# A hybrid RWKV-7/GLA layer on one core: the triangles of a head pair get their own products and their own tile

## The chip, the cores and the metric

The program runs on one core of a Trainium2 chip. The metric is the device time of one execution in microseconds. The engines are TensorE (PE, with its weight loads shown apart as PEld), VectorE (DVE), ScalarE (ACT), GpSimd (POOL) and the queue that issues the DMAs (SP).

## What is computed

One layer over 256 latent tokens and 256 context tokens of width 2048. After a modulated norm, one wide projection feeds two branches. The part that matters here is the RWKV-7 branch, 16 heads of width 64, in both directions:

```
def step(s, inp):                       # S <- S diag(w) + (S a) b^T + v k^T,  y = S r
    w_t, k_t, v_t, a_t, b_t = inp[:5]
    sa = jnp.einsum("bhvk,bhk->bhv", s, a_t)
    s = s * w_t[:, :, None, :] + sa[..., None] * b_t[:, :, None, :] + v_t[..., None] * k_t[:, :, None, :]
    y = jnp.einsum("bhvk,bhk->bhv", s, inp[5]) if emit else None
    return s, y
```

It runs over the context first and then, from the state reached, over the latents. Behind it come a norm per head, a gate, one projection for each branch (`w_a`, `w_b`), a gated sum, the output projection `w_out` and a last norm.

## The kernel before

**Three stages.** First the modulation, the wide projection and the GLA branch; then the RWKV-7 stage, which is what the change touches; then a tail that is almost only matmuls: 16 jobs with `w_b`, 16 with `w_a`, and `w_out`.

**The RWKV-7 stage.** The recurrence is done in chunks of 64 tokens, eight of them (0 to 3 context, 4 to 7 latent), for a pair of heads at a time; there are eight pairs, p = 0 to 7. Inside a chunk the recurrence is a unit lower triangular system, so each chunk, head and direction needs the inverse of a 64x64 triangle. For each pair there are these tracks:

- `fe_track`: the features: `kn`, `ar` (the a vectors and r, scaled), `bk` (the b vectors and k, scaled). Its second half starts when the products of the pair before are done (`("gg", p-1)`), and `ar` is written when `aq_track` of the pair before has read it.
- `gg_track`: the products of `bk` with `ar`, masked by DVE into `GM` (`pgc` for the context chunks, `pgl` for the latent ones). `GM` has two buffers, used by even and odd pairs. So each group of products waits for the scan two pairs back to have passed the chunks concerned (`past(p, i)`), the last one until its last chunk is done.
- `inv_track`: the inverses. ACT copies the triangles from `GM` into `Lin` (four copies), DVE transposes `Lin` into `M`, and POOL substitutes: 30 times a multiply into `tm` and an add into `M`, one after the other. Then DVE transposes `M` back into `Lin`, PE makes the off-diagonal block (`pH`, then `pZ`), and the result is copied into `Z`. It starts when `("gg", p)` is done.
- `aq_track`: DMAs that put part of `ar` into the rows of `GM` from which the triangles have been read.
- `sc_track`: the scan, eight steps. A step is `p1` on PE, a copy, `pU` on PE, a copy into `UV`, `pSs` on PE, then `Sn` on DVE and a copy. In the four latent steps PE adds to `pY`, and `mu`, a reduction of `pY` on DVE, ends the scan. Scans follow each other strictly, and scan p needs `Z` of pair p.

**What sets the order.** Tracks are generators. `Issue` keeps a clock for each engine from its own costs for each instruction, takes the track that can go first, and emits its instructions. So every engine has one fixed queue and works it off in that order. Between the small matmuls of the tracks it places dense ones, `acc` (three matmuls of 128x256 at a time: weights split in a high and a low part by ACT, `wH`, and DVE, `wL`): first the rest of the wide projection, and when the last pair's products and features are issued (`"C"`), the `w_b` jobs. What of the dense work finds no place beside the scans comes behind them.

The planner's price of a POOL operation is in `Op.__init__`; of the hand-over between two engines, in `LAT`:

```
            c = 35 + 0.83 * n if name == "memset" else 110 + 3.36 * n if name == "tensor_copy" else 149 + (
                1.667 if any(q == 0 and k > 1 for x in ins for q, k in x.ap[1:]) else 2.096) * n
```

Of the kernel before, what the change touches and what calls it, by code (L numbers as in the profile page):

```python
# [7 lines left out]
F32 = mybir.dt.float32  # L8
# [4 lines left out]
OP = mybir.AluOpType  # L13
# [4 lines left out]
P = 128  # L18
# [312 lines left out]
def hybrid_layer(tc, a, out):  # L331
    nc = tc.nc
    es = ExitStack()
    with es:
# [635 lines left out]
        def half(hd):  # L970
            return slice(64 * hd, 64 * hd + 64)
# [7 lines left out]
        def fe_track(p, fp, xp):  # L979

            yield lambda: p == 0 or ("feat", p - 1) in DONE
            wl = fp.tile([P, 2, 2, P], F32, name="wl", tag="wl", bufs=1)
            for i, nm in enumerate(("a_w2", "a_a2")):
                for hf in range(2):
                    Q.dma_start(wl[half(hf), i], a[nm][0][:, :, P * p:P * p + P].rearrange("d r c -> r d c"))
# [107 lines left out]
        def bt_track(p, d, bk):  # L1093
# [8 lines left out]
                rel(pt)  # L1102
            DONE.add(("bt", p) if ("bt", p, 1 - d) in DONE else ("bt", p, d))

        def gg_track(p, fp, xp):

            yield lambda: ("feat", p) in DONE
            s = RW[p]
            ar, bks = s["ar"], s["bks"]
            GM, GMr, BK = s["GM"], s["GMr"], s["BK"] = tuple(RW[n][p % 2] for n in ("GM", "GMr", "BK"))  # L1110
            left = [6]

            def done():
                left[0] -= 1
                if not left[0]:
                    DONE.add(("gg", p))

            def mask(m, n):
                return m[:, p % 2, None].to_broadcast([P, n, 2, 64])

            def ev_c(pg, hd):
                yield DV.tensor_tensor(GM[:, hd, 0:4], pg, mask(m_ab, 4), op=OP.mult)
                rel(pg)
                done()

            def ev_l(pg, hd, i):
                yield DV.tensor_tensor(GM[:, hd, 4 + i:6 + i], pg[:, :, :, 0, :], mask(m_ab, 2), op=OP.mult)
                yield DV.tensor_tensor(GMr[:, hd, i:i + 2], pg[:, :, :, 1, :], mask(m_r, 2), op=OP.mult)
                rel(pg)
                done()  # L1130

            yield past(p, 3)
            pg = []
            for hd in range(2):
                pg.append((yield Claim("g3", [P, 4, 2, 64], f"pgc{hd}", *bks, ar)))
            yield [PE.matmul(pg[hd][half(x), i, d, :], bks[d][half(hd), chunk(i, d), x, :], ar[half(hd), d, i, 0, :],
                             start=True, stop=True) for i in range(4) for d in range(2) for x in range(2) for hd in range(2)]
            for hd in range(2):
                iss.spawn(3, ev_c(pg[hd], hd), "evc")
            for i in (0, 2):  # L1140
                yield past(p, 5 + i)
                pg = []
                for hd in range(2):
                    pg.append((yield Claim("g3", [P, 2, 2, 2, 64], f"pgl{hd}", *bks, ar)))
                yield [PE.matmul(pg[hd][:, ii, d], bks[d][half(hd), chunk(4 + i + ii, d)].rearrange("p a b -> p (a b)"),
                                 ar[half(hd), d, i + ii, 1:3, :], start=True, stop=True)
                       for ii in range(2) for d in range(2) for hd in range(2)]
                for hd in range(2):
                    iss.spawn(3, ev_l(pg[hd], hd, i), "evl")

        def inv_track(p, fp, xp):

            yield lambda: ("gg", p) in DONE and (p < 2 or ("gi", p - 2) in DONE)
            s = RW[p]
            GM, Z = s["GM"], RW["Z"][p % 2]
            h0 = u0 = 64 * (p % 2)
            hs = slice(h0, h0 + 64)  # L1160
            qs = [slice(h0 + 32 * hd, h0 + 32 * hd + 32) for hd in range(2)]
            Lin, M, GMo = (RW[n][hs] for n in ("Lin", "M", "GMo"))
            for hd in range(2):
                for blk in range(2):
                    r = slice(u0 + 32 * blk, u0 + 32 * blk + 32)
                    cc = slice(32 * blk, 32 * blk + 32)
                    yield AC.copy(RW["Lin"][qs[hd]].rearrange("p t u -> p u t")[:, 16 * blk:16 * blk + 16, :],
                                  GM[r, hd, :, :, cc].rearrange("p i d t -> p (i d) t"))
            yield DV.transpose(M.rearrange("p i c -> p (i c)"), Lin.rearrange("p t u -> p (t u)"))
            for hd in range(2):  # L1170
                yield AC.copy(RW["GMo"][qs[hd]], GM[u0:u0 + 32, hd, :, :, 32:64].rearrange("p i d t -> p (i d) t"))
            iss.spawn(3, aq_track(p, xp), "aq")
            for j in range(1, 31):
                n = 31 - j
                tm = fp.tile([P, 256], F32, name="tm", tag="tm", bufs=2)
                tv = tm[hs, 0:n * j].rearrange("p (a b) -> p a b", b=j)
                yield PO.tensor_tensor(tv, M[:, j + 1:32, j:j + 1].to_broadcast([64, n, j]),
                                       M[:, j:j + 1, 0:j].to_broadcast([64, n, j]), op=OP.mult)
                yield PO.tensor_tensor(M[:, j + 1:32, 0:j], M[:, j + 1:32, 0:j], tv, op=OP.add)
            yield PO.memset(M.rearrange("p i c -> p (i c)")[:, ::33], 1.0)  # L1180
            yield DV.transpose(Lin.rearrange("p u c -> p c u"), M.rearrange("p i c -> p c i"))
            pH = yield Claim("g3", [P, 16, 32], "pH", Lin)
            hq = int(4)
            for u in range(0, 16, hq):
                yield [PE.matmul(pH[q, u + x, :], RW["GMo"][q, u + x, :], RW["Lin"][q, u + x, :], start=True, stop=True,
                                 tile_position=(q.start, q.start)) for x in range(hq) for q in qs]
            yield AC.copy(GMo, pH[hs])
            rel(pH)
            W = RW["Lin"].rearrange("p a b -> p (a b)").rearrange("p (i u) -> p u i", u=32)
            yield DV.transpose(W[hs].rearrange("p u i -> p i u"), M)  # L1190
            pZ = yield Claim("g3", [P, 16, 32], "pZ", GMo, Lin)
            for u in range(0, 16, hq):
                yield [PE.matmul(pZ[64 * hd:64 * hd + 32, u + x, :], RW["GMo"][qs[hd], u + x, :], W[qs[hd], 16 + u + x, :],
                                 start=True, stop=True, tile_position=(qs[hd].start, 64 * hd)) for x in range(hq) for hd in range(2)]
            yield lambda: p < 2 or ("sc1", p - 2) in DONE
            for hd in range(2):
                for blk in range(2):
                    r = slice(64 * hd + 32 * blk, 64 * hd + 32 * blk + 32)
                    yield (DV.tensor_copy if hd else AC.copy)(Z[r, :, 32 * blk:32 * blk + 32], W[qs[hd], 16 * blk:16 * blk + 16, :])
                yield (DV.tensor_copy if hd else AC.copy)(Z[64 * hd:64 * hd + 32, :, 32:64], pZ[64 * hd:64 * hd + 32])  # L1200
            rel(pZ)
            s["Z"] = Z
            DONE.add(("gi", p))

        def aq_track(p, xp):

            s = RW[p]
            ar, GM, rq = s["ar"], s["GM"], RW["rq"]
            us = rows(p)[0]
            for hd in range(2):  # L1210
                for g in range(2):
                    for d in range(2):
                        yield DM.dma_start(GM[us, hd, 4 * g:4 * g + 4, d, :], ar[half(hd), d, :, g, :])
                yield DM.dma_start(rq[us, :, :, hd, :], ar[half(hd), :, :, 2, :])
            DONE.add(("aq", p))

# [417 lines left out]
        fp = Pool(iss, fes.enter_context(tc.tile_pool(name="rwf", bufs=1, side="right", reuse_waits="tile")))  # L1634
        ies = ExitStack()
        ip = Pool(iss, ies.enter_context(tc.tile_pool(name="rwi", bufs=1, reuse_waits="tile")))
        for n, sh in (("Lin", [P, 32, 32]), ("M", [P, 32, 32]), ("GMo", [P, 16, 32])):
            RW[n] = iss.keep(ip.tile(sh, F32, name=n))
        RW["ar"] = iss.keep(xp.tile([P, 2, 4, 3, 64], F32, name="ar"))
        RW["rq"] = iss.keep(xp.tile([P, 2, 4, 2, 64], F32, name="rq"))  # L1640
        for n, sh in (("GM", [P, 2, 8, 2, 64]), ("BK", [P, 2, 8, 2, 64]), ("GMr", [P, 2, 4, 2, 64])):
            RW[n] = [iss.keep(xp.tile(sh, F32, name=f"{n}{i}")) for i in range(2)]
        RW["wlo"] = iss.keep(fp.tile([P, 2, 2, P], F32R, name="wlo"))
        G.memset(RW["wlo"].bitcast(F32), 0.0)
        RW["UV"] = iss.keep(xp.tile([P, 8, 2, 2, 64], F32, name="UV"))
# [4 lines left out]
        for p in range(8):  # L1650
            iss.spawn(3.2, fe_track(p, fp, xp), f"fe{p}")
            iss.spawn(3, v_track(p, ip), f"v{p}")
            iss.spawn(6, gg_track(p, ip, xp), f"gg{p}")
            iss.spawn(3, inv_track(p, ip, xp), f"inv{p}")
            iss.spawn(4, mv_track(p, ip, xp), f"mv{p}")
            iss.spawn(2, sc_track(p, xp), f"sc{p}")
# [129 lines left out]
```

## Time and profile before

| what | us |
|---|---|
| median of three runs (1376.9 to 1382.26) | 1380.76 |
| the profiled execution | 1380.07 |
| its span, first to last instruction | 1378.3 |
| PE busy | 1268.4 |
| DVE busy | 963.3 |
| POOL busy | 557.5 |

The span is what the trace shows; 1.8 us of the profiled execution lie around it. A busy time is the time in which the engine had an instruction running. The RWKV-7 stage lies between about 590 and 1213 us, the tail behind it.

### The profile page before, as it was taken

The page shows a single profiled execution, that of the slowest core. Times are in us where ns is not written, and L with a number is a line of the kernel's source. Part 1 is how long each engine was busy: PE and PEld are TensorE (multiplying, and loading weights), DVE is VectorE, ACT ScalarE, POOL GpSimd, SP SyncE. Part 2 cuts the span into 40 slices and gives each one's busy share as a digit, 9 for nine tenths or more (in the row PEclk, how much of TensorE's full clock was granted, in tenths as well). Part 3 has the DMA queues.
Part 4 walks back from the last instruction along what each step waited for, and adds up shares of the span by engine and source line. Part 5 has one row for each costly group of instructions (what it writes and reads, how often), then busy time and mean ns, then how long its engine had stood idle before and what let it go on. Part 6 is the DMA issues. An engine that isn't in the chain of part 4 may idle for free.

```text
span 1378.3 us, 29069 instructions
## 1 busy us (share of the span) xinstructions
PE 1268.4 (92%) x11223; PEld 1063.4 (77%) x11223; DVE 963.3 (70%) x2013; ACT 716.3 (52%) x1449; POOL 557.5 (40%) x684
## 2 busy tenths in 40 slices
PE   5999989999999999999888999798879899999996
PEld 3555579788788898998777778677768688899876
DVE  4433496875965747776986889579866876677656
ACT  5222244343434534486486767475847575544444
POOL 0000476776560000006785569547763855000002
PEclk9999999999999999999999999799989999999999
DMA  9999465455562533666543434243434253578574
GB/s 346 344 336 307 130 204 173 131 177 160 153 177 81 144 92 108 167 182 172 138 111 109 109 98 121 75 104 109 108 82 107 72 160 114 165 208 255 179 245 142
DMA packets 311182, 220.40 MB, mean 160 GB/s; under 512 B 37354, under 2 KB 286724, under 8 KB 310532
## 3 DMA queue, kind: packets, MB, share of 16 engines
q1 hardware_dynamic: 311044, 218.55, 54.4%
q8 instruction: 88, 1.44, 0.4%
q14 instruction: 50, 0.41, 0.1%
HBM read 199.76 MB, written 12.46 MB: 154 GB/s over the span
## 4 chain that ended last, share of the span: by engine, by line
PE 55%; DVE 17%; POOL 11%; ACT 7%; issue 5%; DMA 4%; SPq 1%; DVEq 0%; ACTq 0%; POOLq 0%
PE acc L304 35%; POOL M L304 6%; PE pv L304 6%; DVE wL L304 5%; POOL tm L304 5%; PE pg L304 3%; ACT Lin L304 2%; DMA raw<-in_w_out_dram 2%; ACT wH L304 2%; PE pS L304 1%; PE pout L304 1%; PE pgl L304 1%; DVE bk L304 1%; PE pU L304 1%; PE p L304 1%
## 5 line engine op out<-in xcount | busy, mean ns | idle before, releaser
L304 DVE TENSOR_TENSOR wL<-raw,wH 128x512 fp32r<-128x512 f32 x484 | 379.2, 792 | 166.3 <-ACT wH L304 157.8
L304 ACT CAST wH<-raw 128x512 fp32r<-128x512 f32 x484 | 293.9, 615 | 330.7 <-PE acc L304 204.4
L304 PE MATMUL acc<-lH,wH 128*128 128x256 f32 x896 | 287.6, 321 | 0.5 <-ACT tg L304 0.5
L304 PE MATMUL acc<-lH,wL 128*128 128x256 f32 x896 | 259.0, 289 | 0.9 <-DVE wL L304 0.9
L304 PE MATMUL acc<-lL,wH 128*128 128x256 f32 x896 | 258.9, 289 | 0.0
L304 POOL TENSOR_TENSOR tm<-M 64x30 f32<-64x30 f32 (+14 forms) x240 | 165.2, 688 | 153.0 <-DVE M L304 74.4
L304 PEld LDWEIGHTS acc<-lH,wH 128*128 128x128 f32 x896 | 177.0, 198 | 20.8 <-issue 5.7
L304 POOL TENSOR_TENSOR M<-M,tm 64x30 f32<-64x30 f32 (+14 forms) x240 | 180.0, 750 | 18.7
L304 PEld LDWEIGHTS acc<-lL,wH 128*128 128x128 f32 x896 | 177.6, 198 | 4.5 <-issue 3.0
L304 PEld LDWEIGHTS acc<-lH,wL 128*128 128x128 f32 x896 | 177.1, 198 | 1.3 <-DVE wL L304 1.3
L304 PE MATMUL acc<-hH,wH 128*128 128x512 f32 (+1 forms) x416 | 169.0, 406 | 1.0 <-ACT lo L304 1.0
L304 PE MATMUL acc<-hH,wL 128*128 128x512 f32 (+1 forms) x416 | 157.6, 379 | 0.0
L304 PE MATMUL acc<-hL,wH 128*128 128x512 f32 (+1 forms) x416 | 157.2, 378 | 0.0
L304 PEld LDWEIGHTS acc<-hH,wH 128*128 128x128 f32 x416 | 78.7, 189 | 38.0 <-issue 22.9
L304 POOL TENSOR_TENSOR gw<-gw,csl 128x512 f32<-128x512 f32 x60 | 73.7, 1229 | 64.7 <-DMA gw<-in_w_mod_dram 64.7
L304 POOL TENSOR_TENSOR xs<-yg,fg 128x512 f32<-128x512 f32 (+1 forms) x10 | 13.5, 1366 | 198.3 <-DVE yg L304 198.3
L304 PEld LDWEIGHTS acc<-hH,wL 128*128 128x128 f32 x416 | 78.8, 189 | 15.4 <-DVE wL L304 0.4
L304 POOL TENSOR_TENSOR ga<-ga,gw 128x512 f32<-128x512 f32 x60 | 86.0, 1434 | 4.2
L304 PEld LDWEIGHTS acc<-hL,wH 128*128 128x128 f32 x416 | 79.1, 190 | 10.5 <-DVE hL L304 0.4
L304 PE MATMUL acc<-yH,wH 128*128 128x256 f32 x256 | 76.2, 298 | 2.0 <-DVE mt L304 1.9
L304 PE MATMUL acc<-yH,wL 128*128 128x256 f32 x256 | 72.7, 284 | 0.0
L304 PE MATMUL acc<-yL,wH 128*128 128x256 f32 x256 | 72.7, 284 | 0.0
(314 smaller groups left out, 2594.2 us busy)
## 6 DMA issues: line engine op xcount, KB each, us to landing
raw<-in_w_in_dram SPq DMA_DIRECT2D x174, 512.0 KB, 4.0
wm<-in_w_mod_dram SPq DMA_DIRECT2D x64, 512.0 KB, 7.0
gw<-in_w_mod_dram SPq DMA_DIRECT2D x64, 256.0 KB, 4.1
raw<-in_w_out_dram SPq DMA_DIRECT2D x32, 512.0 KB, 4.4
raw<-in_w_b_dram SPq DMA_DIRECT2D x16, 512.0 KB, 3.9
raw<-in_w_a_dram SPq DMA_DIRECT2D x16, 512.0 KB, 5.2
kv<-kvo SPq DMA_DIRECT2D x16, 256.0 KB, 3.7
tg<-tg SPq DMA_DIRECT2D x32, 128.0 KB, 3.7
```

The source lines that it names most:

```text
L304: op = Op("dma" if name == "dma_start" else self.key, name, lambda: f(*a, **k), aps[0], aps[1:], func, k.get("accum_out"), any(x.tensor.na ...
```

## The change

A new track, `ab_track`, makes the products of which the triangles are cut (`bk` and `ar` of the same head, all eight chunks) into a tile of their own, `AB`, as soon as the features of the pair are there and the triangles of the pair before have been copied out of `AB`. `inv_track` reads `AB` and no longer `GM`, and starts when `AB` is there. `gg_track` follows behind `ab_track`; its context products leave out the half that now goes through `AB`. `aq_track` no longer waits for the inverse to have read `GM`, but for the scan two pairs back, like the products. To make room, `wl` shares the buffers of `t0` and `tm` has one buffer.

```diff
-            wl = fp.tile([P, 2, 2, P], F32, name="wl", tag="wl", bufs=1)
+            wl = iss.tile(fp, [P, 2, 2, P], F32, "wl", "t0", 2)
...
+        def ab_track(p, xp):
+
+            yield lambda: ("feat", p) in DONE and (p == 0 or ("lin", p - 1) in DONE)
+            ar, bks = RW[p]["ar"], RW[p]["bks"]
+            AB = RW["AB"]
+            xb = p % 2
+            for g in range(2):
+                pa = yield Claim("g3", [P, 4, 2, 64], "pab", *bks, ar)
+                yield [PE.matmul(pa[half(hd), i, d, :], bks[d][half(hd), chunk(4 * g + i, d), xb, :], ar[half(hd), d, i, g, :],
+                                 start=True, stop=True) for i in range(4) for d in range(2) for hd in range(2)]
+                yield DV.tensor_tensor(AB[:, 4 * g:4 * g + 4], pa, RW["m_t"][:, None, None, :].to_broadcast([P, 4, 2, 64]), op=OP.mult)
+                rel(pa)
+            DONE.add(("ab", p))
...
-            yield lambda: ("feat", p) in DONE
+            yield lambda: ("ab", p) in DONE
...
-            yield [PE.matmul(pg[hd][half(x), i, d, :], bks[d][half(hd), chunk(i, d), x, :], ar[half(hd), d, i, 0, :],
-                             start=True, stop=True) for i in range(4) for d in range(2) for x in range(2) for hd in range(2)]
+            yield [PE.matmul(pg[hd][vs, i, d, :], bks[d][half(hd), chunk(i, d), xk, :], ar[half(hd), d, i, 0, :],
+                             start=True, stop=True) for i in range(4) for d in range(2) for hd in range(2)]
...
+            iss.spawn(3, aq_track(p, xp), "aq")
...
-            yield lambda: ("gg", p) in DONE and (p < 2 or ("gi", p - 2) in DONE)
+            yield lambda: ("ab", p) in DONE and (p < 2 or ("gi", p - 2) in DONE)
...
-                                  GM[r, hd, :, :, cc].rearrange("p i d t -> p (i d) t"))
+                                  AB[r, :, :, cc].rearrange("p i d t -> p (i d) t"))
...
-            iss.spawn(3, aq_track(p, xp), "aq")
+            DONE.add(("lin", p))
+            yield lambda: p == 0 or ("sub", p - 1) in DONE
...
-                tm = fp.tile([P, 256], F32, name="tm", tag="tm", bufs=2)
+                tm = fp.tile([P, 256], F32, name="tm", tag="tm", bufs=1)
...
+            DONE.add(("sub", p))
...
-            for hd in range(2):
-                for g in range(2):
+            for g in range(2):
+                yield past(p, 3 + 4 * g)
+                for hd in range(2):
...
-        for n, sh in (("Lin", [P, 32, 32]), ("M", [P, 32, 32]), ("GMo", [P, 16, 32])):
+        for n, sh in (("Lin", [P, 32, 32]), ("M", [P, 32, 32]), ("GMo", [P, 16, 32]), ("AB", [P, 8, 2, 64])):
```

The planner makes a new order of it on every engine. On DVE, the transpose `M<-Lin` is the last thing that POOL needs before it can start on a pair's inverse, and the first `Lin<-M` (64x32x32) needs POOL's last result. Before, the `M<-Lin` of pair 2 stood behind the first `Sn` of scan 1 (the `Sn` rows without `SD`; the `xc` row closes the norm of scan 0):

```order
L304 TENSOR_SCALAR Sn<-pSs,Dt 128x64 x2
L304 TENSOR_TENSOR xc<-xc,rl_i 128x256
L304 COPY UV<-Sn 64x2x64
L304 STREAM_TRANSPOSE M<-Lin 64x1024
L304 TENSOR_TENSOR wL<-raw,wH 128x512
```

Now it stands within scan 0, ahead of the `Lin<-M` of pair 1:

```order
L304 SCALAR_TENSOR_TENSOR Sn<-pSs,Dt,SD 128x64 x2
L304 STREAM_TRANSPOSE M<-Lin 64x1024
L304 COPY UV<-Sn 64x2x64
L304 TENSOR_TENSOR GM_6075<-pgl_8209,m_ab 64x256
L304 TENSOR_TENSOR GMr_6079<-pgl_8209,m_r 128x256
L304 TENSOR_TENSOR GM_6075<-pgl_8210,m_ab 64x256
L304 TENSOR_TENSOR GMr_6079<-pgl_8210,m_r 128x256
L304 STREAM_TRANSPOSE Lin<-M 64x32x32
```

The pair 2 transpose moved ahead by three scan steps and past the transpose back of pair 1. Counted in scan steps (rows `Sn`, eight to a scan) that stand ahead of it in DVE's queue, `M<-Lin` of the pairs 2 to 7 stood at 9, 16, 25, 32, 41, 48 and now stands at 6, 17, 24, 32, 38, 47; the first `Lin<-M` of the pairs 1 to 7 stood at 6, 16, 21, 32, 38, 48, 56 and now stands at 6, 13, 23, 29, 38, 45, 55. Scan p begins at 8p.

On PE, the last rows of the scan of pair 7 and what follows them. Before, the dense rows around them were of the `w_b` jobs (`acc<-yH`, `acc<-yL`):

```order
L304 MATMUL acc<-yH_13752,wL 128x256
L304 MATMUL pSs<-UV,BK_6077 64x64 x4
L304 MATMUL pY<-UV,GMr_6079 64x64 x4
L304 MATMUL acc<-yH_13752,wH 128x256
L304 MATMUL acc<-yL_13753,wH 128x256
```

Now they are of the wide projection (`acc<-lH`, `acc<-lL`):

```order
L304 MATMUL acc<-lH,wL 128x256
L304 MATMUL pSs<-UV,BK_6078 64x64 x4
L304 MATMUL pY<-UV,GMr_6080 64x64 x4
L304 MATMUL acc<-lH,wH 128x256
L304 MATMUL acc<-lL,wH 128x256
L304 MATMUL acc<-lH,wL 128x256
```

Behind the last scan step there were 504 `acc` matmuls and there are now 816; ahead of it there are 312 fewer. The total is the same. The 480 matmuls with `w_out` follow in both.

On DVE, from the `mu` of scan 0 to that of scan 6, there were 665 instructions and are 667: 12 `wL` fewer, 10 `AB` and 5 `rc` more, and three others.

## Rows read from the trace of the kernel before

**Rows 1.** The page: span, busy time and share of two engines.
```profile
span 1378.3 us, 29069 instructions
PE 1268.4 (92%) x11223; PEld 1063.4 (77%) x11223; DVE 963.3 (70%) x2013; ACT 716.3 (52%) x1449; POOL 557.5 (40%) x684
```
**Rows 2.** One tile: the reduction that ends each of the eight scans.
```profile
L304 DVE TENSOR_REDUCE mu<-pY x8: 412/415/424, 760.5 to 1212.6; 128x4 f32<-128x256 f32 x8
```
**Rows 3.** Windows cut at the ends of the scans, and one of the tail.
```profile
core 0: us, PE busy (x) PEld busy (x) DVE busy (x) ACT busy (x) POOL busy (x), PEclk, DMA share, GB/s
...
760.50:817.10 56.60, 50.54 (x594) 43.01 (x593) 50.67 (x112) 38.23 (x88) 40.95 (x57) 1.00 0.41 106
817.10:900.50 83.40, 72.62 (x920) 62.41 (x918) 60.08 (x126) 55.44 (x110) 50.72 (x71) 0.88 0.35 93
900.50:950.80 50.30, 45.30 (x487) 37.69 (x486) 44.67 (x101) 37.20 (x87) 35.13 (x48) 1.00 0.42 105
950.80:1044.10 93.30, 79.86 (x1025) 68.57 (x1024) 68.78 (x141) 57.21 (x116) 57.62 (x81) 0.89 0.36 92
1044.10:1104.40 60.30, 52.17 (x581) 43.83 (x580) 50.71 (x106) 38.74 (x89) 40.63 (x61) 0.94 0.42 108
1104.40:1159.80 55.40, 52.65 (x650) 45.87 (x649) 38.56 (x87) 36.92 (x86) 39.01 (x61) 0.94 0.50 139
1159.80:1212.60 52.80, 51.77 (x663) 45.60 (x662) 37.36 (x96) 30.58 (x76) 0.00 (x0) 1.00 0.53 152
1225.00:1250.00 25.00, 25.00 (x213) 25.00 (x212) 19.11 (x41) 12.63 (x25) 0.00 (x0) 1.00 0.93 268
```
**Rows 4.** Waits of POOL and of DVE, 632 to 1163 us: total, times, longest.
```profile
POOL tm L304 <- DVE M L304: 74.4, 6, 25.7
POOL tm L304 <- DVE rl_i L304: 30.6, 1, 30.6
...
DVE kn L304 <- ACT rs L304: 17.1, 6, 4.9
DVE Lin L304 <- POOL M L304: 17.0, 3, 6.6
```
**Rows 5.** Timeline of POOL (start, length): edges of the inverses 0, 1, 2, 7.
```profile
633.17 0.61 POOL L304 TENSOR_TENSOR tm<-M 64x30 f32<-64x30 f32 x1 [6.38 <-DVE M L304]
...
691.46 0.75 POOL L304 TENSOR_TENSOR tm<-M 64x30 f32<-64x30 f32 x1 [7.79 <-DVE M L304]
744.62 0.16 POOL L304 MEMSET M<- 64x32 f32 x1
770.47 0.61 POOL L304 TENSOR_TENSOR tm<-M 64x30 f32<-64x30 f32 x1 [25.68 <-DVE M L304]
819.22 0.15 POOL L304 MEMSET M<- 64x32 f32 x1
1115.91 0.25 POOL L304 TENSOR_TENSOR tm<-M 64x30 f32<-64x30 f32 x1 [15.89 <-DVE M L304]
1159.39 0.15 POOL L304 MEMSET M<- 64x32 f32 x1
```
**Rows 6.** Groups of one tile: ns min/median/max, first and last start.
```profile
L304 DVE TENSOR_TENSOR GM<-pgl,m_ab x32: 404/416/425, 623.4 to 1109.9; 128x256 f32<-128x256 f32 x32
L304 ACT COPY Lin<-GM x32: 1040/1113/1167, 627.2 to 1113.5; 32x512 f32<-32x512 f32 x32
L304 DVE TENSOR_TENSOR GM<-pgc,m_ab x16: 670/677/693, 621.0 to 1092.8; 128x512 f32<-128x512 f32 x16
```
**Rows 7.** Groups by shape: PE in 632:1163, wL in 632:686, wL in 1175:1225.
```profile
L304 PE MATMUL pZ<-Lin,GMo 32*32 32x32 f32 x448 | 14.3, 228 | 1.2 <-ACT GMo L304 1.2
L304 PE MATMUL pgc<-ar,bk 64*64 64x64 f32 x448 | 8.4, 221 | 0.0
...
L304 DVE TENSOR_TENSOR wL<-raw,wH 128x512 fp32r<-128x512 f32 x24 | 22.6, 948 | 1.7 <-ACT wH L304 1.6
...
L304 DVE TENSOR_TENSOR wL<-raw,wH 128x512 fp32r<-128x512 f32 x23 | 15.9, 690 | 6.3 <-ACT wH L304 5.9
```

More of the change, by code (lines that the diff above doesn't have):

```diff
@@ L1110, in gg_track @@
             GM, GMr, BK = s["GM"], s["GMr"], s["BK"] = tuple(RW[n][p % 2] for n in ("GM", "GMr", "BK"))
+            vs = rows(p)[1]
+            xk = 1 - p % 2
             left = [6]
@@ L1116, in done, with mask @@
                     DONE.add(("gg", p))
-            def mask(m, n):
-                return m[:, p % 2, None].to_broadcast([P, n, 2, 64])
+            def mask(m, n, r):
+                return m[r, p % 2, None].to_broadcast([r.stop - r.start, n, 2, 64])
             def ev_c(pg, hd):
-                yield DV.tensor_tensor(GM[:, hd, 0:4], pg, mask(m_ab, 4), op=OP.mult)
+                yield DV.tensor_tensor(GM[vs, hd, 0:4], pg[vs], mask(m_ab, 4, vs), op=OP.mult)
                 rel(pg)
@@ L1126, in ev_l @@
             def ev_l(pg, hd, i):
-                yield DV.tensor_tensor(GM[:, hd, 4 + i:6 + i], pg[:, :, :, 0, :], mask(m_ab, 2), op=OP.mult)
-                yield DV.tensor_tensor(GMr[:, hd, i:i + 2], pg[:, :, :, 1, :], mask(m_r, 2), op=OP.mult)
+                yield DV.tensor_tensor(GM[vs, hd, 4 + i:6 + i], pg[vs, :, :, 0, :], mask(m_ab, 2, vs), op=OP.mult)
+                yield DV.tensor_tensor(GMr[:, hd, i:i + 2], pg[:, :, :, 1, :], mask(m_r, 2, slice(0, P)), op=OP.mult)
                 rel(pg)
@@ L1151, in inv_track @@
         def inv_track(p, fp, xp):
-            yield lambda: ("gg", p) in DONE and (p < 2 or ("gi", p - 2) in DONE)
+            yield lambda: ("ab", p) in DONE and (p < 2 or ("gi", p - 2) in DONE)
             s = RW[p]
-            GM, Z = s["GM"], RW["Z"][p % 2]
-            h0 = u0 = 64 * (p % 2)
+            AB, Z = RW["AB"], RW["Z"][p % 2]
+            h0 = 64 * (p % 2)
             hs = slice(h0, h0 + 64)
@@ L1164, in inv_track @@
                 for blk in range(2):
-                    r = slice(u0 + 32 * blk, u0 + 32 * blk + 32)
+                    r = slice(64 * hd + 32 * blk, 64 * hd + 32 * blk + 32)
                     cc = slice(32 * blk, 32 * blk + 32)
                     yield AC.copy(RW["Lin"][qs[hd]].rearrange("p t u -> p u t")[:, 16 * blk:16 * blk + 16, :],
-                                  GM[r, hd, :, :, cc].rearrange("p i d t -> p (i d) t"))
+                                  AB[r, :, :, cc].rearrange("p i d t -> p (i d) t"))
             yield DV.transpose(M.rearrange("p i c -> p (i c)"), Lin.rearrange("p t u -> p (t u)"))
             for hd in range(2):
-                yield AC.copy(RW["GMo"][qs[hd]], GM[u0:u0 + 32, hd, :, :, 32:64].rearrange("p i d t -> p (i d) t"))
-            iss.spawn(3, aq_track(p, xp), "aq")
+                yield AC.copy(RW["GMo"][qs[hd]], AB[64 * hd:64 * hd + 32, :, :, 32:64].rearrange("p i d t -> p (i d) t"))
+            DONE.add(("lin", p))
+            yield lambda: p == 0 or ("sub", p - 1) in DONE
             for j in range(1, 31):
                 n = 31 - j
-                tm = fp.tile([P, 256], F32, name="tm", tag="tm", bufs=2)
+                tm = fp.tile([P, 256], F32, name="tm", tag="tm", bufs=1)
                 tv = tm[hs, 0:n * j].rearrange("p (a b) -> p a b", b=j)
@@ L1209, in aq_track @@
             us = rows(p)[0]
-            for hd in range(2):
-                for g in range(2):
+            for g in range(2):
+                yield past(p, 3 + 4 * g)
+                for hd in range(2):
                     for d in range(2):
                         yield DM.dma_start(GM[us, hd, 4 * g:4 * g + 4, d, :], ar[half(hd), d, :, g, :])
+            for hd in range(2):
                 yield DM.dma_start(rq[us, :, :, hd, :], ar[half(hd), :, :, 2, :])
@@ L1642, in hybrid_layer @@
             RW[n] = [iss.keep(xp.tile(sh, F32, name=f"{n}{i}")) for i in range(2)]
+        m_t = ip.tile([P, 64], F32, name="m_t")
+        for hf in range(2):
+            V.tensor_copy(m_t[half(hf)], m_ab[half(hf), hf, 0, :])
+        RW["m_t"] = m_t
         RW["wlo"] = iss.keep(fp.tile([P, 2, 2, P], F32R, name="wlo"))
@@ L1652, in hybrid_layer @@
             iss.spawn(3, v_track(p, ip), f"v{p}")
+            iss.spawn(3, ab_track(p, xp), f"ab{p}")
             iss.spawn(6, gg_track(p, ip, xp), f"gg{p}")
```

## The prediction, made before the run

> **What bounds the kernel now.** I read the page first: PE is busy for 92% of the span and is the fullest engine [rows 1]. So a change that leaves the sum of the matmuls as it is can win only where PE idles or runs at the lower clock. Then I cut the RWKV-7 stage at the eight `mu` reductions that end the scans [rows 2] and read the windows between them [rows 3]. The intervals alternate. Those of the scans 1, 3 and 5 take 56.6, 50.3 and 60.3 us, those of the scans 2 and 4 take 83.4 and 93.3, and the last two, which have no more features beside them, 55.4 and 52.8. In the short ones DVE is busy for 50.67, 44.67 and 50.71 us, together 146.05 of 167.2 or 87%; in the two long ones for 60.08 and 68.78, which is 72% and 74%. PE is at 86 to 90% in both kinds, but in the long ones its granted clock falls to 0.88 and 0.89: part of its busy time there is the lower of its two levels, 1.2 GHz.
>
> The long intervals are the even pairs, which have to wait for their inverse. The waits of POOL show it: 25.68 us idle ahead of the inverse of pair 2, 30.6 ahead of a later one, 15.89 ahead of pair 7 [rows 4, 5]. POOL waits for the transpose, that for the copies, these for `GM`, and `GM` for the scan two pairs back. An inverse then takes 43.6 us (pair 7), 48.9 (pair 2) or 53.3 (pair 1) on POOL [rows 5]. Three times the wait is the other way round: DVE stands at `Lin<-M` until POOL is done, 17.0 us in all [rows 4], and everything behind it in DVE's queue, the scan's copies among it, stands too.
>
> **The start.** Before, ACT's copies begin at 627.2 us, behind the two `pgc` groups (masked from 621.0) and the first `pgl` groups (from 623.4) [rows 6]. Now they need two groups of `pab` and two maskings of the size of the `pgc` ones, 0.68 us each. That leaves out the `pgl` groups and their maskings: about 5 us less (bounds 0 and 6.2, the distance from 621.0 to 627.2). **-5.**
>
> **The scans 1 to 5.** Here the change works: it puts the inverses of the even pairs beside the scans. What is then left is DVE's work. From the end of scan 0 to that of scan 6 its queue holds 665 instructions before and 667 now. 12 `wL` fewer save about 10 us (at 0.69 to 0.95 each [rows 7]), 10 `AB` add 6.8 (0.677 each, by `GM<-pgc` [rows 6]), 5 `rc` add little: the same work within 2 us. In the five intervals DVE was busy for 274.9 of 343.9 us [rows 3]. At the 87.4% of the undisturbed three that is 314.5 us. **-29**, if no new wait comes. Bounds: 0, if the order only shifts the waits, and -45 at the 92% that 274.9 in 299 would be (the best single interval shows 89.5%).
>
> **The waits that stay.** POOL needs the same time for an inverse. DVE comes to `Lin<-M` after a number of scan steps that can be counted in the order. Before, the inverses with 6, 5 and 6 steps between `M<-Lin` and `Lin<-M` (pairs 1, 3 and 5) are the three that made DVE wait; those with 7 steps (2, 4, 6) did not. That fits the lengths: 6 steps at 56.6/8 = 7.1 us are 42 us, 7 steps 50, and POOL wants 49 to 53. Now pair 1 has 6 steps as before, and pairs 3, 4 and 5 have 6, 5 and 6; pairs 2 and 6, with 7, can only start on POOL when pairs 1 and 5 are through. So three waits of 17.0/3 = 5.7 us fall into the intervals that I have just counted without any. Bounds: 0 and 25 us, four and more such waits. Part of one is caught up behind it, since ACT and PE work on; I take **+13**, nearer to the three full waits than to nothing.
>
> **The last two scans.** Pair 6 no longer waits after scan 5, and 8 dense triples fewer stand beside scan 7: **-3** together. Pair 7's `Lin<-M` comes after 55 steps, one before scan 7 begins, where it came after 56: its inverse still ends after scan 6 and its wait stays.
>
> So the last scan ends at about 1212.6 - 5 - 29 + 13 - 3 = 1189 us.
>
> **What comes back behind it.** 312 `acc` matmuls more stand behind the last scan step. In the tail PE has no idle time and does 213 of them in 25.00 us [rows 3], 0.1174 us each: **+37**. Nothing hides it, since PE is the engine that ends last there. These are w_b jobs and one job of the gates, and DMA is at 0.93 and 268 GB/s in that window [rows 3]; a few stalls for `raw` would add to it (bound +5).
>
> **Costs at nothing.** PE does 16 matmuls more for each pair: `pab` with two places of the array in use, as `pZ` (14.3/7 = 2.0 us a pair), in place of half of `pgc` (8.4/7 = 1.2) [rows 7], so 0.6 to 1.4 us, 5 to 11 in all. They are covered, since 312 dense matmuls, 37 us, have left the same stretch; without that cover they would cost all of it. `aq_track`'s DMAs are as many as before and go out earlier. `tm` in one buffer costs nothing: POOL does multiply and add in turn anyway. `wl` in the ring of `t0` makes `rs` (ACT) wait for POOL's reads of `wl`; in POOL's queue these stand between two inverses or late within one, and are done before `rs` needs them while POOL is on time. That is a price in the third rival.
>
> **The sum.** -5 - 29 + 13 - 3 + 37 = +13 us on the profiled execution's 1380.07 (span 1378.3 and 1.8 around it), whose time is 0.7 under the median of the runs: 1393 us. The mechanism works and the stage gets shorter by 24 us. But its idle time was where dense matmuls ran, and these come back at full price.
>
> **Rivals.** *Faster:* no wait for POOL appears and DVE goes at 90 to 92%. For it: the interval of scan 1, 89.5% with an inverse beside it, and the low clock of the long intervals, which would go too. Against it: it needs POOL to be done after 5 or 6 steps, which it never was. At 92% it gives -5 - 45 - 3 + 37 = -16, 1364 us; it decides from about -37 on in the scans 1 to 5, where the total is -8.
>
> *No change:* the waits are caught up except for a third of them, +0 to +6 in place of +13: the stage gives back what the tail takes, 1380 to 1387 us. For it: the two amounts, 32 to 37 and 37, are almost the same, and both stem from the same dense work.
>
> *Slower still:* inverses get longer because they lie over a fuller DVE. For it: 43.6 us where DVE is busy for 70% (38.56 of 55.4), 48.9 where it is at 89.5% [rows 3, 5]; `wL` takes 690 ns with POOL at rest and 948 beside an inverse [rows 7]. Then the inverses with 7 steps make DVE wait as well, five or six times 5.7 us, and the reads of `wl` come late for `rs`, for which DVE's `kn` waited 17.1 us already [rows 4]. +25 to +35 in place of +13: 1405 to 1415 us. The Trainium skill has a rule for this in "SBUF — State Buffer", section "Who interferes with whom": a DVE instruction with two SBUF inputs contends with a GpSimd instruction that reads SBUF, and the order of issue decides which of them waits. The trace agrees as far as the two `wL` rows go. By that rule every inverse would come to the 53 us end, the time of this rival.
>
> *The change doesn't do it:* the inverse of pair p still needs the features of pair p, these the products of pair p-1, and these the scan p-3. In scan steps `M<-Lin` moves from 9, 16, 25, 32, 41, 48 to 6, 17, 24, 32, 38, 47, never by more than 3. If the scans gain nothing by that, -5 - 0 - 3 + 37 is 1409, within the rival above.
>
> **How the numbers follow.** Chances: the forecast 0.42 (its own range 1388 to 1402), no change 0.27, faster 0.20, slower still 0.11. A measurement of this kernel can tell about 0.5%, 7 us, from no change. So faster 0.20, same 0.27, slower 0.53. The range leaves out half of the faster case and half of the slowest: 1368 to 1407.
>
> **What would show it.** In the changed profile: `mu` of scan 0 about 5 us earlier; the intervals of the scans 2 and 4 no longer 25 to 30 us longer than their neighbours; DVE's wait at `Lin<-M` for POOL still 15 to 25 us; last `mu` near 1189; then 37 us more of dense matmuls at full rate. I am wrong if the last `mu` comes before 1175 (then it is faster), if DVE hardly waits for POOL, or if the tail takes its 312 matmuls in clearly more or less than 37 us.

## The result, and the profile after

The changed kernel takes **1363.38 us** (median of three runs, 1361.36 to 1364.38) where the kernel before took 1380.76. The ratio is 0.9865 [0.9817, 0.9912]. So it is faster by 17 us, 0.9 to 1.8%, and the prediction of 1393 us, slower, was wrong in sign. The profiled execution took 1361.36 us, its span 1359.6.

The page of the changed kernel, to be held against [rows 1]:

```profile
span 1359.6 us, 29662 instructions
PE 1270.1 (93%) x11479; PEld 1068.1 (79%) x11479; DVE 968.3 (71%) x2031; ACT 718.2 (53%) x1449; POOL 543.3 (40%) x684
```

PE has 256 matmul rows more (16 matmuls more for each of the eight pairs, and the trace shows each of them in two rows) and is busy for 1.7 us more. No work has gone; 18.7 us of the span have. The ends of the scans (one tile, as in [rows 2]):

```profile
L304 DVE TENSOR_REDUCE mu<-pY x8: 405/415/420, 748.1 to 1159.1; 128x4 f32<-128x256 f32 x8
```

The windows cut at these ends, as in [rows 3] (columns as there), with one of the tail:

```profile
748.10:797.30 49.20, 46.05 (x608) 38.86 (x607) 46.25 (x108) 33.55 (x82) 26.79 (x41) 1.00 0.38 92
797.30:860.10 62.80, 53.88 (x696) 45.84 (x695) 50.96 (x116) 41.73 (x93) 49.03 (x67) 0.96 0.46 117
860.10:936.30 76.20, 70.78 (x965) 60.50 (x962) 65.64 (x137) 53.91 (x108) 41.42 (x64) 0.94 0.40 100
936.30:1009.50 73.20, 66.22 (x784) 56.41 (x781) 59.22 (x128) 55.23 (x110) 62.91 (x92) 0.88 0.36 92
1009.50:1067.70 58.20, 54.01 (x727) 45.82 (x726) 48.24 (x110) 39.34 (x88) 24.39 (x41) 0.97 0.32 83
1067.70:1113.00 45.30, 43.70 (x519) 37.48 (x519) 33.94 (x78) 26.94 (x73) 35.74 (x55) 1.00 0.57 147
1113.00:1159.10 46.10, 45.96 (x598) 39.90 (x592) 29.51 (x80) 29.05 (x76) 0.00 (x0) 1.00 0.50 136
1175.00:1200.00 25.00, 25.00 (x211) 25.00 (x210) 15.74 (x27) 10.90 (x18) 0.00 (x0) 1.00 0.81 237
```

The last `mu` starts at 1159.1 us, 53.5 earlier than before; the tail behind it is 200.5 us long in place of 165.7. Of the 53.5 us, 12.4 are won by the end of scan 0, 24.3 in the scans 1 to 5 (319.6 us for 343.9) and 16.8 in the last two (91.4 for 108.2). The tail takes 34.8 back.

**The seams.** What the prediction didn't do is to look at each seam: from the `mu` that ends a scan to the first `pU` of the next, which needs `Z`, the finished inverse. In the kernel before, scan 6 shows one in the timeline (start, length):

```profile
1119.68 0.69 DVE L304 COPY Z<-pZ 32x512 f32<-32x512 f32 x1 [0.91 <-ACT Z L304]
...
1120.83 0.69 PE L304 MATMUL pU<-R,Z 64*64 64x64 f32 x8
```

Scan 5 had ended at 1104.40 [rows 3]. The last piece of `Z` is ready at 1120.4, and `pU` starts 0.5 us later: a seam of 16.4 us, in which the inverse is what comes last. The seam of scan 1, whose `Z` is ready before scan 0 ends, takes 4.5 us, so about 12 of the 16.4 us are the price of the late inverse. It began late: ahead of the inverse of pair 6 POOL stood idle for 30 us.

```profile
1054.76 0.32 POOL L304 TENSOR_TENSOR tm<-M 64x30 f32<-64x30 f32 x1 [30.06 <-DVE rl_t L304]
```

The timeline of the changed kernel:

```profile
860.13 0.42 DVE L304 TENSOR_REDUCE mu<-pY 128x4 f32<-128x256 f32 x1
...
874.98 0.69 DVE L304 COPY Z<-pZ 32x512 f32<-32x512 f32 x1
...
877.67 1.28 ACT L304 ACT_TABLE_LOAD   x1 [1.34 <-issue]
878.97 0.69 ACT L304 ACTIVATE rs<-pq,e 128x512 f32<-128x512 f32 x1
...
879.52 0.45 PE L304 MATMUL p<-UV,GM 64*64 64x64 f32 x8
...
879.67 1.28 ACT L304 ACT_TABLE_LOAD   x1
880.97 0.63 ACT L304 ACTIVATE rs<-rs 128x512 f32<-128x512 f32 x1
881.51 0.55 ACT L304 ACTIVATE yt<-pyt,vec 128x256 f32<-128x256 f32 x1
881.96 0.25 ACT L304 COPY R<-p 128x128 f32<-128x128 f32 x1
...
885.51 0.45 PE L304 MATMUL pU<-R,Z 64*64 64x64 f32 x8
...
1057.27 0.69 DVE L304 COPY Z<-pZ 32x512 f32<-32x512 f32 x1 [2.41 <-ACT Z L304]
...
1067.66 0.41 DVE L304 TENSOR_REDUCE mu<-pY 128x4 f32<-128x256 f32 x1
...
1072.25 0.45 PE L304 MATMUL pU<-R,Z 64*64 64x64 f32 x8
...
1113.03 0.41 DVE L304 TENSOR_REDUCE mu<-pY 128x4 f32<-128x256 f32 x1
...
1120.30 0.69 DVE L304 COPY Z<-pZ 32x512 f32<-32x512 f32 x1 [0.20 <-ACT Z L304]
...
1121.43 0.45 PE L304 MATMUL pU<-R,Z 64*64 64x64 f32 x8
```

At 1058.0 the inverse of pair 6 is ready 9.7 us before scan 5 ends; the seam is 4.6 us, about the shortest of this kernel. That of scan 7 is 8.4 us, still with `Z` as what comes last (1121.0). All the seams, read in this way, in us:

| before scan | 1 | 2 | 3 | 4 | 5 | 6 | 7 | sum |
|---|---|---|---|---|---|---|---|---|
| before | 4.5 | 23.4 | 5.0 | 32.2 | 5.0 | 16.4 | 14.1 | 100.6 |
| changed | 4.6 | 4.9 | 25.4 | 15.1 | 3.6 | 4.6 | 8.4 | 66.6 |

From the first `mu` to the last the stage is 41.1 us shorter, and 34.0 of that are seams. The change took away the wait of the scans 2, 4 and 6 for their inverse. But a new seam has come at scan 3. There `Z` is late by 15.5 us (875.7 against 860.1). Then `p`, the first product of the scan, comes on PE at 879.5, its copy `R` stands in ACT's queue behind `rs` of the next features and the table loads until 881.96, 2 us after `p` is done, and `pU` comes on PE 3.3 us after `R`. The 15.1 us of scan 4 have another cause than the inverse: its `Z` is ready at 930.9, 5.4 us before scan 3 ends. On ACT `rs` with its two table loads runs from 944.71 to 948.64, then come the copies `UV<-pV`, then `p` (949.58) and `pU` (951.40). That this queue sets the seam is read from the trace and was not tested.

### The profile page after: what moved, and what is told of

Read it like the earlier page. It is cut to its first block, busy times and chain, and to the rows that moved or that the text cites. A ratio compares the mean times of both kernels' runs of the same rounds, so it can differ in the third digit from the quotient of the medians.

```text
span 1359.6 us, 29662 instructions
## 1 busy us (share of the span) xinstructions
PE 1270.1 (93%) x11479; PEld 1068.1 (79%) x11479; DVE 968.3 (71%) x2031; ACT 718.2 (53%) x1449; POOL 543.3 (40%) x684
## 5 line engine op out<-in xcount | busy, mean ns | idle before, releaser
L304 PE MATMUL acc<-lL,wH 128*128 128x256 f32 x896 | 256.0, 286 | 0.0
L304 PE MATMUL acc<-lH,wL 128*128 128x256 f32 x896 | 255.6, 285 | 0.2 <-DVE wL L304 0.2
L304 PEld LDWEIGHTS acc<-lH,wH 128*128 128x128 f32 x896 | 173.4, 194 | 21.1 <-issue 4.5
L304 POOL TENSOR_TENSOR tm<-M 64x30 f32<-64x30 f32 (+14 forms) x240 | 160.1, 667 | 74.3 <-DVE M L304 48.1
L304 POOL TENSOR_TENSOR M<-M,tm 64x30 f32<-64x30 f32 (+14 forms) x240 | 170.1, 709 | 18.7
L304 PEld LDWEIGHTS acc<-lL,wH 128*128 128x128 f32 x896 | 174.5, 195 | 3.1 <-issue 1.7
L304 PEld LDWEIGHTS acc<-lH,wL 128*128 128x128 f32 x896 | 173.9, 194 | 0.4 <-DVE wL L304 0.4
L304 PEld LDWEIGHTS acc<-hH,wH 128*128 128x128 f32 x416 | 78.6, 189 | 38.1 <-issue 22.9
L304 PEld LDWEIGHTS acc<-hH,wL 128*128 128x128 f32 x416 | 78.4, 188 | 15.5 <-DVE wL L304 0.4
L304 PE MATMUL acc<-yH,wH 128*128 128x256 f32 x256 | 73.0, 285 | 0.0
```

Of the source, the lines that this page charges most:

```text
L304: op = Op("dma" if name == "dma_start" else self.key, name, lambda: f(*a, **k), aps[0], aps[1:], func, k.get("accum_out"), any(x.tensor.na ...
```

## The experiments

All times are medians; each ratio, with its 95% interval, is to the kernel before, run beside it, whose median was 1380.46 to 1382.02 us in the four sets of runs. The lengths of scans and seams come from one profiled execution of each kernel.

**The wait put back, for all pairs and for parts.** The new products and the tile stay; only the start of `inv_track` waits as it did before. For the second kernel only the pairs 6 and 7 wait, for the third only 2 to 5.

```diff
-            yield lambda: ("ab", p) in DONE and (p < 2 or ("gi", p - 2) in DONE)
+            yield lambda: ("ab", p) in DONE and ("gg", p) in DONE and (p < 2 or ("gi", p - 2) in DONE)
...
+            yield lambda: ("ab", p) in DONE and (p < 6 or ("gg", p) in DONE) and (p < 2 or ("gi", p - 2) in DONE)
...
+            yield lambda: ("ab", p) in DONE and (p in (0, 1, 6, 7) or ("gg", p) in DONE) and (p < 2 or ("gi", p - 2) in DONE)
```

> The changed kernel in which the inverse of a pair waits again for all products of its pair, and so for the scan two pairs back; products, tile and rings of the change stay. If the gain comes from the scans that no longer wait for an inverse, it goes: 600 dense matmuls stand behind the last scan step instead of 816, 25 us less of tail, and the stage grows by the 53 us it had won less some 5 for the start: 1383 us, plus or minus 8. If it comes from the other parts (rings, products, a tile of its own), the time stays at 1360 to 1368.

> The changed kernel with that wait put back for the pairs 6 and 7 alone. The intervals of the scans 6 and 7 were 17 us shorter than before. If that came from their inverses, they are 108 us together again, 756 dense matmuls behind the scan save 7 us of tail, and the time is 1373, plus or minus 5. If those intervals got shorter because features and dense matmuls beside them went away, it stays at 1358 to 1366.

> The changed kernel with that wait put back for the pairs 2 to 5 alone. The intervals of the scans 1 to 5 were 24 us shorter than before. If that came from the inverses of the pairs 2 and 4, they are 344 us again, 750 matmuls behind the scan save 8 us, and the time is 1379, plus or minus 6. If the pairs 6 and 7 carry the gain, it is 1362 to 1368.

Measured: all pairs 1376.85 us, 0.9989 [0.9963, 1.0016]; pairs 6 and 7 1372.13, 0.9951 [0.9926, 0.9975]; pairs 2 to 5 1373.89, 0.9964 [0.994, 0.9989]. All three times lie in the ranges that the wait gave, but they differ by no more than orders of one structure do (see below), so the lengths of the stage and of the seams have to decide. With the wait on all pairs the last `mu` is late again:

```profile
L304 DVE TENSOR_REDUCE mu<-pY x8: 403/415/419, 759.3 to 1202.6; 128x4 f32<-128x256 f32 x8
```

Its seams are 12.2, 22.9, 3.8, 19.8, 7.2, 15.4 and 11.0, with large ones at 2, 4, 6 and 7 as before and one more at 1. So the early start of the inverses, not the tile or the product order by itself, shortens the stage. But 600 `acc` matmuls stand behind the last scan step there, 96 more than before (11 us), though the stage is no shorter than in other orders of before. With the wait on pairs 6 and 7 alone the timeline shows the two seams come back:

```profile
1073.98 0.42 DVE L304 TENSOR_REDUCE mu<-pY 128x4 f32<-128x256 f32 x1
...
1087.40 0.69 DVE L304 COPY Z<-pZ 32x512 f32<-32x512 f32 x1 [1.23 <-ACT Z L304]
...
1089.89 0.39 PE L304 MATMUL pU<-R,Z 64*64 64x64 f32 x6
...
1128.12 0.41 DVE L304 TENSOR_REDUCE mu<-pY 128x4 f32<-128x256 f32 x1
...
1139.77 0.69 DVE L304 COPY Z<-pZ 32x512 f32<-32x512 f32 x1
...
1141.54 0.37 PE L304 MATMUL pU<-R,Z 64*64 64x64 f32 x6
```

1074.0 to 1089.9 and 1128.1 to 1141.5 are 15.9 and 13.4 us, and the last two scans take 106.5 us, not 91. The seams 1 to 4 stay within 1.6 us of those of the changed kernel; seam 5 is 8.2 us, where it was 3.6. Against the changed kernel run again later, on another chip (span 1361.8), the last two scans cost 15.2 us, the start 5.4 (another order), and the tail gives 9.3 back; the span is 1373.2. The scans 1 to 5 stay (317.2 and 317.0).

With the wait on the pairs 2 to 5 the time was as expected, but the way to it was not. The seams 2 and 4 come back (22.3 and 22.9 us). Still, the scans 1 to 5 take 324.6 us together, not 344: seam 3 falls to 8.0, and the time outside the seams is about 255 us, where it was 266. And the last two scans, whose pairs don't wait, take 100.3 us. So it is shown that the wait makes the seams 2 and 4; that it makes the 24 us of the scans 1 to 5 is not.

**The rings alone**, in the kernel before (`wl` in the ring of `t0`, `tm` with one buffer):

```diff
-            wl = fp.tile([P, 2, 2, P], F32, name="wl", tag="wl", bufs=1)
+            wl = iss.tile(fp, [P, 2, 2, P], F32, "wl", "t0", 2)
...
-                tm = fp.tile([P, 256], F32, name="tm", tag="tm", bufs=2)
+                tm = fp.tile([P, 256], F32, name="tm", tag="tm", bufs=1)
```

> The kernel before with the two small edits of the change alone: wl in the ring of t0 and tm in one buffer. The wait theory expects no change: 1375 to 1386. If one buffer of tm is what made POOL's inverses shorter (47 us a piece after, 49 before), POOL is busy for 543 us instead of 557 and the time is 1366 to 1372; if the ring costs rs a wait, it is above 1387.

1374.55 us, 0.9954 [0.9933, 0.9976]: 6 us faster, between the range of no change and that of a shorter POOL. POOL is busy for 558.2 us, so the one buffer of `tm` doesn't shorten the inverses. Every queue has a different order. The large seams at 2 and 4 stay (24.5 and 26.3 us), but seam 5 is 19.5 us where it was 5.0, seam 6 is 8.4 where it was 16.4, and seam 7 is 21.7 where it was 14.1. That raised the question of what the order by itself is worth.

**The same work in other orders.** The planner's price for a hand-over from ACT (`LAT`, 135 in both kernels) is changed by a few units. It changes no instruction's work, only the choices and so the order. First for the whole program, in both kernels, with the changed kernel run again beside them:

```diff
-    LAT = {"pe": 200.0, "act": 135.0, "dve": 135.0, "pool": 135.0, "dma": 920.0}
+    LAT = {"pe": 200.0, "act": 137.0, "dve": 135.0, "pool": 135.0, "dma": 920.0}
```

> The changed kernel once more, beside the next three on one chip: 1363, plus or minus 4, ratio 0.984 to 0.990 with a narrower interval than that of three runs.

> The kernel before with nothing changed but the planner's price of a hand-over by ACT, 137 in place of 135: the same work in a slightly different order (528 dense matmuls behind the scan, 504 before). If a new order by itself moves the time by as much as the two rings did (6 us), this moves it by 3 to 8 us one way or the other; if the rings did it by what they hold, this stays within 2 us of the kernel before.

> The changed kernel with the same new price (864 dense matmuls behind the scan, 816 without it). If the gain is the change's, 1363 plus or minus 7; if it was one lucky order, 1372 or more.

Then from the RWKV-7 stage on, with 129, 131, 133 and 137 in each of the kernels:

```diff
         state["b0"] = iss.small
+        iss.LAT = dict(iss.LAT, act=131.0)
```

> The kernel before with the planner's price of ACT's hand-over at 131 from the start of the RWKV-7 stage on, so the same work in another order. Luck of the order: somewhere in 1364 to 1382, as the two orders measured so far (1381, 1366). If 1381 is what this structure takes, 1377 to 1385.

> The changed kernel with the same price. If the change itself wins 17 us, 1356 to 1369 and at least 10 under its twin. If part of the 17 is luck of the order, 1362 to 1377, and the twins differ by 5 or so. The intervals of the scans 1 to 5 are 315 to 325 us together in either case (336 to 344 in the twin), and the tail 35 to 43 us longer than the twin's.

> As the first, with 133: 1364 to 1382 by luck of the order, 1377 to 1385 without it.

> As the second, with 133: at least 10 under its twin if the change itself wins 17 us; within 0 to 10 of it if most of that was the order.

> The kernel before, planner's price of ACT's hand-over 129 from the RWKV-7 stage on. If orders alone scatter the time, 1364 to 1382, mean 1372.

> The changed kernel with 129. If orders alone decide, 1362 to 1378 on either side of its twin; if the change itself wins, under its twin by 10.

> The kernel before with 137 in this stage alone: 1364 to 1382. The order with 137 in the whole program took 1366.

> The changed kernel with 137 in this stage alone: 1362 to 1378; in the whole program 137 gave 1376. If that order of the stage is the slow one, 1372 or more again.

| order | structure of before, us | ratio | changed structure, us | ratio |
|---|---|---|---|---|
| as it was | 1380.76 | | 1363.38; again 1362.89 | 0.9848 [0.9817, 0.9879] |
| 137, whole program | 1365.89 | 0.9888 [0.9869, 0.9906] | 1375.54 | 0.9951 [0.9932, 0.997] |
| 129 | 1367.69 | 0.9885 [0.9842, 0.9928] | 1374.91 | 0.9947 [0.9925, 0.997] |
| 131 | 1374.93 | 0.9947 [0.992, 0.9973] | 1368.81 | 0.991 [0.988, 0.9939] |
| 133 | 1368.63 | 0.9912 [0.9877, 0.9947] | 1373.02 | 0.9951 [0.9932, 0.997] |
| 137 | 1372.14 | 0.9912 [0.9885, 0.9938] | 1374.84 | 0.9952 [0.9922, 0.9983] |
| mean (1363.38 in the first row) | 1371.7 | | 1371.7 | |

The changed kernel's own time repeats. But the kernel before is the slowest of its six orders, and the changed one the fastest of its six. The first new order moved the kernel before by 16 us, more than either expectation allowed. Of the four pairs of twins the changed one is 6 us faster once (131) and 3 to 7 us slower three times; nowhere is it faster by 10. With 131 the scans 1 to 5 take 329.9 us and the tail is 26.6 us longer than the twin's, both outside what was expected. The scatter within a structure is 5.5 and 4.8 us (standard deviation), so the two means are the same within a standard error of 3 us (the root of 5.5²/6 + 4.8²/6). The orders 129 give an example with the other sign, in the span and in the ends of the scans. First the structure of before, the page and one tile:

```profile
span 1365.4 us, 29063 instructions
...
L304 DVE TENSOR_REDUCE mu<-pY x8: 411/415/425, 758.3 to 1203.1; 128x4 f32<-128x256 f32 x8
```

Then the changed one:

```profile
span 1368.1 us, 29671 instructions
...
L304 DVE TENSOR_REDUCE mu<-pY x8: 415/418/426, 749.8 to 1169.6; 128x4 f32<-128x256 f32 x8
```

The last `mu` comes 33.5 us earlier and the span is 2.7 us longer: 162.3 us of tail have become 198.5. What the six profiles of each structure have in common shows by terms (us; means over the six, and the measured pair):

| term | forecast | the pair | mean before | mean changed | difference |
|---|---|---|---|---|---|
| end of scan 0 | -5 | -12.4 | 760.8 | 752.3 | -8.5 |
| scans 1 to 5 | -29 + 13 | -24.3 | 337.1 | 324.3 | -12.8 |
| last two scans | -3 | -16.8 | 106.8 | 89.9 | -16.9 |
| tail | +37 | +34.8 | 166.5 | 202.3 | +35.8 |
| span | +13 | -18.7 | 1371.1 | 1368.8 | -2.3 |

The stage gets shorter in all six: the seams 6 and 7 together are 28.7 us in the mean before and 10.1 with the change, seam 2 falls from 22.9 to 5.1 and seam 4 from 26.5 to 15.4. Seam 3 rises from 6.5 to 25.1 and seam 5 from 8.8 to 14.5. All seams together fall from 99.6 to 74.9 us, so three quarters of the fall are the seams 6 and 7. The tail grows in all six.

**The granted clock.** The order is not all that scatters the time. The 87 executions of the kernel before in the four sets have one order and took 1372.65 to 1389.09 us, with a mean granted clock of TensorE (1 is 2.4 GHz) between 0.974 and 0.958. Where it was 0.969 or more (29 executions) the median is 1379.1 us, where it was 0.962 or less (19) it is 1386.0. The medians of the orders lie the same way for the most part: the kernel before has 0.965, the slowest of its six, and its other orders 0.971 to 0.975; the changed kernel has 0.977 and 0.978 in its two runs, its order 131 has 0.980, and its four slower orders 0.973 to 0.975. So a part of what one order gains on another shows as granted clock. Whether the order brings the clock about was not tested; the kernel before had 0.965 or 0.966 in each of the four sets, which speaks for it.

**A dearer POOL.** In the changed kernel the planner's price of a POOL operation is raised, so that DVE should come to `Lin<-M` later and not wait there:

```diff
-            c = 35 + 0.83 * n if name == "memset" else 110 + 3.36 * n if name == "tensor_copy" else 149 + (
+            c = 35 + 0.83 * n if name == "memset" else 110 + 3.36 * n if name == "tensor_copy" else 400 + (
```

> The changed kernel in which the planner prices a POOL operation on two tiles 251 ns higher, near what it takes (0.69 and 0.75 us against a price of about 0.45). It now puts 8 scan steps where 5 to 7 were between a transpose to POOL and the one back. If DVE's wait for POOL (9.5 us in the changed kernel) still costs time, that wait goes to under 3 us and the time to 1350 to 1358; if those waits are caught up anyway, 1360 to 1368. 372 dense matmuls stand behind the scan, 52 us less of tail than with 816.

1383.61 us, 1.0013 [0.9989, 1.0038]. DVE's wait for POOL is gone, but POOL now waits inside its inverses (total, times, longest):

```profile
POOL wh L304 <- DMA wl<-in_a_a_dram: 131.8, 5, 31.2
```

`wh`, the feature work that the planner put between the steps of an inverse, waits for the load of `wl`, six of the seven seams are 18 to 35 us long, and the last `mu` comes at 1226.9. Neither of the two expected times came. The experiment so doesn't price DVE's wait by itself: one wait was exchanged for a larger one. Whether the load is late because `wl` shares the ring of `t0` was not tried apart.

## Why the prediction was wrong

In the measured pair the sum came out at -18.7 us, not +13. The 31.7 us between them are the last two scans (13.8), the scans 1 to 5 (8.3), the start (7.4) and the tail (2.2). The last `mu`, at 1159.1, comes before the 1175 that the prediction named as its sign of being wrong. But that sign was to mean a faster kernel, and all six changed orders end their scans before 1175 (1159.1 to 1170.6) without being faster in the mean: the tail takes back what the scans give.

**The last two scans: -3 forecast, -16.8 measured.** This step failed. The prediction let pair 6's wait go but took the interval of scan 6, 55.4 us, for a short one, because its neighbours were longer, and never priced the 16.4 us between the `mu` ahead of it and its `pU`. Of POOL's waits it named the 25.68, 30.6 and 15.89 us ahead of the pairs 2, 4 and 7, and left out the 30.06 ahead of pair 6. It also had pair 7's wait stay; it fell from 14.1 to 8.4 us. Putting the wait back on these two pairs alone gives 106.5 us and brings both seams back, so this cause is shown. By the means over the orders, it is nearly all of the miss that belongs to the change itself: +13 forecast, -2.3 measured, 13.9 of it here.

**One order stood for the structure.** The other half of the miss, -18.7 in the pair against -2.3 in the means, is how far these two orders (and the one profiled execution of each) lie from the mean of theirs. The prediction named the new order and read it row by row, but took it that the kernel before stood for its structure. No term and no rival of it stands for the 5 us or so by which a new order alone moves the time here. The mean of the six changed orders, 1371.7 us, would lie in the stated range of 1368 to 1407; the order that was measured doesn't. Why these two orders in particular lie at the ends isn't settled. The granted clock goes with them: the lowest of the six of before, the second highest of the changed six. In the pair, the scans 1 to 5 before (344.0) are the longest of the six of before, and those after (319.6) the shortest of the changed six.

**The scans 1 to 5: -29 + 13 forecast, -24.3 in the pair, -12.8 in the mean.** The size of the sum was near, the way to it wasn't. DVE's share was meant to rise to 87.4%; it is 270.3 of 319.6 us, 84.6%. And no wait was added. The waits of POOL and DVE between 620 and 1163 us, which answer to [rows 4]:

```profile
POOL tm L304 <- DVE M L304: 48.1, 5, 30.8
POOL wh L304 <- PE pgc L304: 35.6, 1, 35.6
POOL wh L304 <- DMA wl<-in_a_a_dram: 25.4, 1, 25.4
...
DVE Lin L304 <- POOL M L304: 9.5, 4, 5.6
DVE kn L304 <- ACT rs L304: 9.2, 3, 4.0
```

DVE waits at `Lin<-M` for 9.5 us in four times, 2.4 us each, where 15 to 25 us were forecast and 17.0 stood before. What was left to win in these scans lies in the seams at 3 (new) and 4 (halved), not in DVE's share. The intervals of the scans 2 and 4 no longer stand out over their neighbours, as was foretold: 62.8 and 73.2 us beside 49.2, 76.2 and 58.2.

**The start: -5 forecast, -12.4 in the pair, -8.5 in the mean.** The copies of the triangles begin 7.4 us earlier than in [rows 6]:

```profile
L304 ACT COPY Lin<-AB x32: 1055/1086/1143, 619.8 to 1062.5; 32x512 f32<-32x512 f32 x32
```

Of these, 3 us were won ahead of the change: in this order the `ar` of pair 0 comes at 613.3 us and not at 616.3. The mechanism was right; the rest lies between the copies and the end of scan 0.

**The tail: +37 forecast, +34.8 measured.** Right, in place and price: PE does 211 matmuls in 25.00 us, where it did 213, and the 312 more cost 34.8 us, 0.112 each. Over all orders the tail follows the number of `acc` matmuls that stand behind the last scan step: 372 with a tail of 152.8 us (the dearer POOL) and 864 with 209.7 (137, whole program), 0.116 us each. The 16 matmuls more for each pair, which the prediction put at nothing as long as they are covered, seem to be paid here too: with the wait on all pairs the stage is that of before and the tail is 178.3 us where the mean of before is 166.5. In the mean over the orders PE is busy for 1273.0 us with the change and for 1264.0 without it, 9 us, of the size of the 5 to 11 us that the prediction priced and then took as covered. That they lengthen the span isn't shown.

**The rivals.** *Faster* gave the time (1364) by luck: DVE didn't reach 92%, and five other orders of the same structure took 1369 to 1376 us. *No change* has the mechanism that the orders bear out: the stage gives what the tail takes, -38 against +36. *Slower still* needed longer inverses. They are shorter, if anything; the edges of the inverses of the pairs 5 and 7, the longest and the shortest of eight:

```profile
939.63 0.24 POOL L304 TENSOR_TENSOR tm<-M 64x30 f32<-64x30 f32 x1 [5.75 <-DVE M L304]
...
991.02 0.15 POOL L304 MEMSET M<- 64x32 f32 x1
...
1065.01 0.25 POOL L304 TENSOR_TENSOR tm<-M 64x30 f32<-64x30 f32 x1 [30.84 <-DVE M L304]
...
1107.44 0.15 POOL L304 MEMSET M<- 64x32 f32 x1
```

51.5 and 42.6 us, against 43.6 to 53.3 before [rows 5], although now more of them lie beside a scan. The rule that the prediction took from "SBUF — State Buffer" of the Trainium skill, section "Who interferes with whom", may hold for single instructions (the two `wL` rows). No run here shows it to lengthen an inverse as a whole.

What stays open: with a standard error of 3 us from six orders each, the change in structure may be worth some 6 us either way. The twelve orders are neighbours of one price, not a random draw. And how much of the scatter between orders comes by the granted clock, and how much by the seams, was not taken apart.

## What to carry to other kernels

Where a planner makes the order, a structural edit also draws a new order. Time some orders of the old and of the new structure (a price moved by a few per cent will do) before the edit is credited with the difference; here the order alone was worth up to 15 us, and the edit, in the mean of six orders, nothing that could be told from zero. Read the granted clock of every execution beside its time. Price each seam, from the end of one step of the chain to the first instruction that needs the late operand, rather than the mean share of an engine. And work that used to fill the gaps comes back behind the stage at its full price, so a shorter stage pays only if its gaps were empty.

## What the runs showed of the hardware that was not expected

- ACT loads a table twice around `rs`, 1.28 us each, and `rs` takes 0.69 and 0.63 us: 3.9 us of ACT in one piece (877.67 to 881.6), of which two thirds are table loads. In the queue of an engine that also does a copy of the scan, such a piece adds to a seam: `p` is done at 879.97 and its copy `R` starts at 881.96.
- Fewer waits did not bring the full clock. In the scans 2 to 5 of the changed kernel the granted clock is 0.96, 0.94, 0.88 and 0.97, so part of that time still runs at 1.2 GHz, and the lowest stands in the window with the long inverse of pair 5 and PE busy for 66.22 of 73.20 us.
